# Branch B weights of three heads as seven block products in place of eight

## The chip, the cores and the metric

The kernel runs on one core of a Trainium2 chip. The metric is device time in microseconds (us) of one execution. A measurement of this kernel tells a change of about 0.2% from none. PE is the matrix engine (TensorE), PEld its weight loads, DVE is VectorE, ACT is ScalarE, POOL is GpSimd, SP the engine that issues most of the DMAs.

## The reference, cut to what matters

One transformer layer on 512 tokens of 1024 features, in float32: two token mixers in parallel (branch A, a gated delta rule; branch B, a retention), a gated sum, an output projection, and an MLP. The change concerns branch B's last step, where the four heads' outputs of 512 features each are multiplied by one weight matrix of 2048 x 1024.

```
ob = chunk_retention(qb, kb, vb)                     # 4 heads x 512 features
ob = rmsnorm(ob, norm_b.reshape(B_HEADS, B_DV)) * jax.nn.silu(gb...)
yb = ob.reshape(b, s, B_V) @ w_br_b                  # [512, 2048] @ [2048, 1024]
mix = (sigmoid(gate_a) * ya + sigmoid(gate_b) * yb) @ w_out
```

## The kernel before

Every matrix product is made of three matmuls: both operands are split into a rounded part `hi` and the rest `lo`, and hi x hi, hi x lo and lo x hi are added up in PSUM. A weight block of 128 x 1024 elements is loaded to a tile `raw`, ACT writes `whi` (L148), and DVE writes `wlo = raw - whi` (L149). `whi` and `wlo` have three buffers each, `raw` has two in each of two pools that take turns.

Stages in order of time: branch A to about 490 us; then four heads of branch B; then gate B, the last head's weights and the output projection to about 1034 us; then the MLP in four groups.

A head h of branch B runs through three functions. `scores(h, rows)` makes Q (48 matmuls), then, for h > 0, turns the rows of head h-1 to features (`features`, L397 transposes on PE into the one PSUM tile `tr`, `split_from` at L382 on ACT and L383 on DVE writes `og`, hi and lo), then K (48 matmuls), each followed by the rotation (L1540 to L1548: four products that read PSUM, two sums, then hi on ACT and lo on DVE, into `qr` and `kr`), then the 24 matmuls of the scores, which read `qr` and `kr` and write PSUM tiles `dl` (three buffers). Then the weights of head h-1: `branch_partial` makes two halves of 512 columns with `token_major`, 48 matmuls each, into the four PSUM tiles `mm`; each result is copied or added to `acc`. Then `outputs(h)` makes values and gates with `seven`.

`seven` is a product by blocks in which seven block products replace eight (Winograd's form). Its sums of weight blocks are made in DRAM beforehand: `BlockSums` copies a block (SP queue) and adds another to it by an accumulating DMA (POOL queue, L135). These jobs are issued one at a time behind weight loads, whenever the planned PE time has moved on by `JOB_US`; between 860 and 985 us of planned time (`REST`) none is. The tile library's scheduler sets the order of the instructions on each engine from their order in the code, priorities and free buffers; each engine then works through its own list.

Of the kernel before, what the change touches and what calls it, by code (L numbers as in the profile page):

```python
# [19 lines left out]
P = 128  # L20
T = 512
# [4 lines left out]
OFF_BA = 6144  # L26
OFF_QB, OFF_KB, OFF_VB, OFF_GB = 6160, 7184, 8208, 10256
OFF_GA, OFF_GBR = 12304, 13328
JOBS_FROM, JOB_US = 70.0, 8.5
SMALL_US, CONV_US, TOK_US, PK_US, INV_US, DB_US = 10.5, 6.5, 2.5, 2.0, 46, 1.2  # L30
VT_US, KS_US, PX_US, PC_US, GATE_US, FEAT_US, INV_PRIO, CONV_PRIO, SMALL_PRIO, KEY_PRIO, DECAY_US, AHEAD, TR_US, REC_PRIO, OUT_PRIO, SUM_PRIO = 2.5, 2.4, 3.5, 2.4, 11.0, 1.0, 0, 600, 800, 600, 20.0, 700, 2.2, 900, 900, 300
DFF = 4096
# [31 lines left out]
def hybrid_block_kernel(ctx: ExitStack, tc: tile.TileContext, a: dict, out: bass.AP):  # L64
    nc = tc.nc
    x_d = a["x"][0]
    w_in = a["w_in"][0]
    w_br = [a["w_br_a"][0], a["w_br_b"][0]]
# [6 lines left out]
    trickle, later_adds = [], []  # L75
# [79 lines left out]
    class BlockSums:  # L155


        def __init__(self, src, c1, c2, tag, full=True):
            def block(kh, c):
                return src[4 * kh * P : 4 * (kh + 1) * P, c : c + 512].rearrange("(k p) c -> p k c", p=P)  # L160
# [3 lines left out]
            self.t = {i: dr.tile([P, 4, 512], F32, tag=f"{tag}{i}", name="sums", bufs=1) for i in self.made}  # L164
            self.parts = []
            trickle.extend((self, i, k) for i in self.made for k in (0, 2))
# [4 lines left out]
        def adds(self):  # L171

            for i, k in ((2, 0), (1, 0), (3, 0), (2, 2), (1, 2), (3, 2), (0, 0), (0, 2)):
                if i not in self.made:
# [53 lines left out]
    def bank(pool):  # L228
        if pool is psx:
            return [psx.tile([P, T], F32, tag="dl", name="dl", bufs=3) for _ in range(2)]  # L230
        return [psm.tile([P, T], F32, tag="mm", name="mm") for _ in range(2)]
# [68 lines left out]
        times(d, "s4", x, True)  # L300
        out(0, 1, d, p1, ALU.add)

    def token_product(quarters, tokens=(0, 1)):

        pinned = []

        def product(pss, x, ks, wts, first):
            wh, wl = wts
            xh, xl = quarters[x]
            for t in tokens:  # L310
                tt = slice(t * P, (t + 1) * P)
                for kk in range(2):
                    k = 2 * ks + kk
                    lhs, rhs = (xh[:, k, tt], xl[:, k, tt]), (wh[:, kk, :], wl[:, kk, :])
                    tick(1536)
                    for i in range(3):
                        m = nc.tensor.matmul(  # L317
                            pss[t], lhs[i // 2], rhs[i % 2],
                            start=first and k + i == 0, stop=k + i == 5, skip_group_check=not first,
                        )  # L320
# [26 lines left out]
    def token_major(src, lhs, c0, kts, krow0=0):  # L347

        pss = [psm.tile([P, T], F32, tag="mm", name="mm") for _ in range(4)]
        for k0 in range(0, kts, 2):  # L350
            wh, wl = weights(src, krow0 + k0, 2, c0, 512)
            for t in range(4):
                tt = slice(t * P, (t + 1) * P)
                for kk in range(2):
                    kt = k0 + kk
                    mm3(
                        pss[t],
                        [x[:, tt] for x in lhs(kt)],
                        (wh[:, kk, :], wl[:, kk, :]),
                        kt == 0,  # L360
                        kt == kts - 1,
                    )
        return pss
# [32 lines left out]
    def transpose(ps, src):  # L396
        nc.tensor.transpose(ps, src, ident)  # L397
# [64 lines left out]
    with tc.tile_pool(name="xp", bufs=2) as xp:  # L462
# [405 lines left out]
    def gated_features(o_t, norms, tb=None):  # L868
# [8 lines left out]
    def branch_partial(w, og, krow0):  # L877
        for half in range(2):
            yield half, token_major(w, lambda kt: [o[:, kt, :] for o in og], half * 512, 4, krow0)

    class Rows2:
        def __init__(self, parts):
# [45 lines left out]
    def acc_rows(t, half):  # L928
        return acc_t[:, t, half * 512 : half * 512 + 512]
# [578 lines left out]
    with tc.tile_pool(name="pb", bufs=1) as pb_:  # L1508
# [41 lines left out]
        def scores(h, rows):  # L1550
            dec = pb_.tile([P, T], F32, tag="dec", name="dec", bufs=2)
            nc.scalar.dma_start(dec, a["c_decay"][h])
            pss = feature_major(w_in, xs, OFF_QB + h * 256, 256, 8)
            og = features(h - 1, rows) if rows else None
            qs, ks = (pb_.tile([P, 2, 2, T], F32R, tag=nm, name=nm) for nm in ("qr", "kr"))
            qs, ks = [qs[:, 0], qs[:, 1]], [ks[:, 0], ks[:, 1]]
            rotary(pss, qs)
            rotary(feature_major(w_in, xs, OFF_KB + h * 256, 256, 8), ks)
            if h == 0:
                ya_marks.append(ya_partial(3, prev))  # L1560
            scs = []
            sall = pb_.tile([P, 2560], F32R, tag="s", name="s")
            done = 0
            for i in range(4):
                t0 = min(i * P, 256)
                n = T - t0
                ps = psx.tile([P, T], F32, tag="dl", name="dl", bufs=3)
                for kk in range(2):
                    mm3(
                        ps[:, :n],  # L1570
                        [ks[j][:, kk, i * P : (i + 1) * P] for j in range(2)],
                        [qs[j][:, kk, t0:T] for j in range(2)],
                        kk == 0,
                        kk == 1,
                    )
# [9 lines left out]
            return scs, og  # L1585

        def features(h, rows):
            return gated_features(rows, lambda f: nb[:, 4 * h + f : 4 * h + f + 1])
# [47 lines left out]

        rows = None
        for h in range(4):
            scs, og = scores(h, rows)
            if h == 0:  # L1640

                def gate_a(t, half, src):
                    ta = tmp("g_t")
                    nc.scalar.activation(ta, src, AF.Tanh, scale=0.5)
                    dst = acc_rows(t, half)
                    nc.vector.scalar_tensor_tensor(dst, ta, 1.0, dst, ALU.add, ALU.mult)

                raw_pools.append((pb_, "ych"))
                gate_unit(ga_sums, OFF_GA, gate_a)
                for t in range(4):  # L1650
                    nc.scalar.dma_start(ya_d[:, t, :], acc_t[:, t, :])
# [385 lines left out]
```

## Time and profile before

| | |
|---|---|
| median of 3 runs | 1326.77 us (1326.51 to 1328.75) |
| profiled execution | 1326.62 us |
| its span, first to last instruction | 1324.8 us |
| PE busy | 1308.9 us (99%) |
| DVE busy | 931.3 us (70%) |
| ACT busy | 668.7 us (50%) |
| POOL busy | 89.7 us (7%) |
| DMA | 223.16 MB |

Time outside the span is 1326.62 - 1324.8 = 1.8 us. A busy PE is work in a pipe: a matmul of 512 columns shows as 390 ns, while one starts about every 227 ns.

### The profile page before, as it was taken

Reading aid. Unit: us, or ns where it says so; the run is one execution under the profiler, and the core shown is the slowest. Engines: PE = TensorE matmul, PEld = TensorE weight load, DVE = VectorE, ACT = ScalarE, POOL = GpSimd, SP = SyncE. Lnnn points to the kernel's source line nnn. Section 1 sums busy time; section 2 is a strip of 40 time slices with the busy share of each in tenths; the row PEclk is TensorE's granted clock in tenths of the full one; section 3 lists DMA queues with packets and bytes.
Section 4 is the critical chain, followed back from the end, with each engine's and each line's share of the span. In section 5 each row is a group of like instructions: output and inputs, shape, how many; then the busy total and the mean of one; then the engine's idle time right before and its main releaser. Section 6 shows DMA issues by size and latency. Waiting matters only on the chain.

```text
span 1324.8 us, 17530 instructions
## 1 busy us (share of the span) xinstructions
PE 1308.9 (99%) x6591; PEld 1085.9 (82%) x6591; DVE 931.3 (70%) x1560; ACT 668.7 (50%) x1168; POOL 89.7 (7%) x95
## 2 busy tenths in 40 slices
PE   9999999999999999999999999999999999999997
PEld 7888787888888878888888888888889888888886
DVE  6889757486666578876567776789685746637478
ACT  5784546455534533544453443465266636355364
POOL 2100100000000001000010000000001000000001
PEclk9999999999999999999999999999999999999999
DMA  5336952476765568887293462545629895859635
GB/s 192 134 112 160 203 132 64 114 181 174 191 161 133 127 178 179 271 253 153 79 260 105 120 214 64 160 157 175 223 82 247 230 256 156 245 154 251 191 119 135
DMA packets 115557, 223.16 MB, mean 168 GB/s; under 512 B 6982, under 2 KB 38896, under 8 KB 114960
## 3 DMA queue, kind: packets, MB, share of 16 engines
q1 hardware_dynamic: 96496, 175.13, 41.3%
q0 software_dynamic: 16944, 40.54, 19.1%
q10 hardware_dynamic: 2032, 6.36, 1.3%
q8 instruction: 52, 0.85, 0.3%
q14 instruction: 33, 0.27, 0.1%
HBM read 216.75 MB, written 72.37 MB: 218 GB/s over the span
## 4 chain that ended last, share of the span: by engine, by line
PE 89%; DVE 6%; ACT 3%; issue 1%; DMA 1%; DVEq 0%; ACTq 0%
PE mm L668 18%; PE mm L317 17%; PE dl L317 11%; PE mm L93 10%; PE mm L95 10%; PE mm L94 10%; PE dl L668 5%; PE tr L397 1%; DVE wlo L149 1%; PE dl L94 1%; PE dl L95 1%; PE dl L93 1%; PE tr L677 1%; PE mm L632 1%; DVE tmp L1061 1%
## 5 line engine op out<-in xcount | busy, mean ns | idle before, releaser
L149 DVE TENSOR_TENSOR wlo<-raw,whi 128x1024 fp32r<-128x1024 f32 x269 | 328.2, 1222 | 204.2 <-ACT whi L148 203.1
L148 ACT CAST whi<-raw 128x1024 fp32r<-128x1024 f32 x269 | 282.6, 1052 | 356.5 <-PE mm L668 71.7
L668 PE MATMUL mm<-actT,whi 128*128 128x512 f32 x448 | 144.5, 403 | 0.0
L317 PE MATMUL mm<-whi,xsum 128*128 128x512 f32 x384 | 120.6, 390 | 0.0
L95 PE MATMUL mm<-hn,wlo 128*128 128x512 f32 (+1 forms) x288 | 105.4, 366 | 0.0
L94 PE MATMUL mm<-hn,whi 128*128 128x512 f32 (+1 forms) x288 | 105.3, 366 | 0.0
L93 PE MATMUL mm<-hn,whi 128*128 128x512 f32 (+1 forms) x288 | 105.3, 366 | 0.0
L668 PEld LDWEIGHTS mm<-actT,whi 128*128 128x128 f32 x448 | 80.6, 188 | 14.8
L668 PE MATMUL mm<-actT,wlo 128*128 128x512 f32 x224 | 87.7, 392 | 0.0
L317 PEld LDWEIGHTS mm<-whi,xsum 128*128 128x128 f32 x384 | 71.8, 188 | 14.9
L317 PE MATMUL mm<-wlo,xsum 128*128 128x512 f32 x192 | 74.8, 390 | 0.0
L317 PE MATMUL dl<-whi,ffq 128*128 128x512 f32 x224 | 71.3, 389 | 0.0
L668 PE MATMUL mm<-whi,og 128*128 128x512 f32 x192 | 62.3, 397 | 0.0
L95 PEld LDWEIGHTS mm<-hn,wlo 128*128 128x128 f32 x288 | 54.3, 189 | 8.8
L93 PEld LDWEIGHTS mm<-hn,whi 128*128 128x128 f32 x288 | 54.3, 189 | 8.7
L94 PEld LDWEIGHTS mm<-hn,whi 128*128 128x128 f32 x288 | 54.3, 189 | 8.7
L668 PE MATMUL mm<-whi,actT 128*128 128x512 f32 x176 | 60.3, 405 | 1.0 <-DVE qf L906 1.0
L317 PE MATMUL dl<-whi,actT 128*128 128x512 f32 x192 | 61.1, 390 | 0.0
L317 PE MATMUL mm<-whi,ffq 128*128 128x512 f32 x192 | 60.9, 389 | 0.0
L1830 DVE TENSOR_TENSOR ffq<-r,ffq 128x512 fp32r<-128x512 f32 (+1 forms) x64 | 39.2, 621 | 28.0 <-ACT ffq L1830 27.9
L135 POOL DMA_DIRECT2D sums<-in_w_in_dram x28 | 32.6, 1164 | 359.8 <-DMA sums<-in_w_in_dram 359.8
L93 PE MATMUL mm<-actT,whi 128*128 128x512 f32 x128 | 51.5, 402 | 0.0
(394 smaller groups left out, 2839.4 us busy)
## 6 DMA issues: line engine op xcount, KB each, us to landing
raw<-in_w_in_dram SPq DMA_DIRECT2D x95, 512.0 KB, 4.9
raw<-sums SPq DMA_DIRECT2D x64, 512.0 KB, 4.4
raw<-in_w_up_dram SPq DMA_DIRECT2D x36, 512.0 KB, 7.2
sums<-in_w_in_dram SPq DMA_DIRECT2D x32, 512.0 KB, 5.2
sums<-in_w_down_dram SPq DMA_DIRECT2D x32, 512.0 KB, 6.9
sums<-in_w_in_dram POOLq DMA_DIRECT2D x28, 512.0 KB, 7.4
raw<-in_w_down_dram SPq DMA_DIRECT2D x24, 512.0 KB, 5.9
sums<-sums POOLq DMA_DIRECT2D x20, 512.0 KB, 8.5
```

The costliest lines, as they stand in the source:

```text
L93: nc.tensor.matmul(ps, lh, rh, start=first, stop=False)
L94: nc.tensor.matmul(ps, lh, rl, start=False, stop=False)
L95: nc.tensor.matmul(ps, ll, rh, start=False, stop=last)
L135: tc.keep_in_program_order(nc.gpsimd.dma_start(dst, src, accum_op=ALU.add))
L148: nc.scalar.copy(hi[:, :n], raw[:, :n])
L149: nc.vector.tensor_tensor(lo[:, :n], raw[:, :n], hi[:, :n], ALU.subtract)
L317: m = nc.tensor.matmul(pss[t], lhs[i // 2], rhs[i % 2], start=first and k + i == 0, stop=k + i == 5, skip_group_check=not first,)
L397: nc.tensor.transpose(ps, src, ident)
L632: pin(nc.tensor.matmul(first_keys[f][:, 256:512], ws[w][:, kk, :], xs[x][:, 2 * j + kk, 256:512], start=False, stop=kk == 1 and i == 2, sk ...
L668: m = tc.keep_in_program_order(nc.tensor.matmul(*args, **kwargs))
L677: tc.keep_in_program_order(nc.tensor.transpose(ps, src, ident if by is None else by))
L1830: return nc.scalar.copy(dst[0], r), nc.vector.tensor_tensor(dst[1], r, dst[0], ALU.subtract)
```

## The change

For heads 0, 1 and 2, `branch_partial` is replaced by `branch_seven`. The head's 512 features and 1024 output columns are cut in two, the 512 tokens too, so that a block product is 256 tokens x 256 features x 512 columns, 12 matmuls. Seven of them make the 84 matmuls of a head, where there were 96. Each takes a weight block of its own (7 splits into `whi` and `wlo` for 4), and its PSUM is added to `acc` before the next product goes to the same tiles (14 operations of 128 x 512 for 8). Two of the seven weight blocks are sums from DRAM, two are summed on DVE (`plus`).

The rows by features leave PSUM as float32 into `full` (ACT alone), which has the buffer of `kr`. From it hi and lo of three quarters (`11`, `12`, `22`, in `og`) and four sums of quarters with their hi and lo (`s1` to `s4`, in `osum`, which have the buffers of `vr`) are made. Head 3 stays as it was.

Six copy jobs and six add jobs come into the list, between those of the heads, and `JOB_US` goes from 8.5 to 7.8.

```diff
-JOBS_FROM, JOB_US = 70.0, 8.5
+JOBS_FROM, JOB_US = 70.0, 7.8
...
-    vg_sums = [BlockSums(w_in, OFF_VB + h * 512, OFF_GB + h * 512, f"vg{h}", False) for h in range(4)]
+    vg_sums, br_sums = [], []
+    for h in range(4):
+        vg_sums.append(BlockSums(w_in, OFF_VB + h * 512, OFF_GB + h * 512, f"vg{h}", False))
+        if h < 3:
+            br_sums.append(BlockSums(w_br[1][4 * h * P : 4 * (h + 1) * P, :], 0, 512, f"br{h}", False, 2))
...
-    for sums in [z_sums, ga_sums] + vg_sums + [gb_sums] + down_sums:
+    in_turn = [s for pair in itertools.zip_longest(vg_sums, br_sums) for s in pair if s]
+    for sums in [z_sums, ga_sums] + in_turn + [gb_sums] + down_sums:
...
-            og = features(h - 1, rows) if rows else None
+            xq = branch_quarters(h - 1, rows) if rows else None
...
+        def branch_quarters(h, rows):
+            full = pb_.tile([P, 4, T], F32, tag="kr", name="full")
+            og = [act.tile([P, 4, T], F32R, tag="og", name="og") for _ in range(2)]
+            sums = [pb_.tile([P, 2, 2, 2, 256], F32R, tag=f"vr{i}", name="osum") for i in range(2)]
+            for f in range(4):
+                ps = psx.tile([P, 4, P], F32, tag="tr", name="tr", bufs=1)
+                for t in range(4):
+                    transpose(ps[:, t, :], rows.feature(t, f))
+                n = 4 * h + f
+                nc.scalar.activation(
+                    full[:, f, :], ps.rearrange("p t c -> p (t c)"), AF.Copy, scale=nb[:, n : n + 1]
+                )
...
+            def halved(name, src, pair):
+                nc.scalar.copy(pair[0], src)
+                nc.vector.tensor_tensor(pair[1], src, pair[0], ALU.subtract)
...
+            for name, src, kh, th in (("11", a11, 0, 0), ("12", a12, 1, 0)):
+                halved(name, src, [part(w, kh, th) for w in og])
+            xq["22"] = [part(w, 1, 1) for w in og]
+            nc.scalar.copy(xq["22"][0], a22)
+            nc.vector.tensor_tensor(xq["22"][1], a22, xq["22"][0], ALU.subtract)
+            nc.vector.tensor_tensor(a22, a21, a22, ALU.subtract)
+            nc.vector.tensor_tensor(a21, a11, a21, ALU.subtract)
+            nc.vector.tensor_tensor(a11, a22, a11, ALU.subtract)
+            nc.vector.tensor_tensor(a12, a12, a11, ALU.add)
+            for i, src in ((2, a11), (1, a22), (3, a21), (4, a12)):
+                w = sums[(i - 1) // 2][:, (i - 1) % 2]
+                halved(f"s{i}", src, [w[:, 0], w[:, 1]])
...
+        def branch_seven(h, xq):
+            sums, product = br_sums[h], token_product(xq, kts=2)
...
+            x, y = sums.first_raw(1, 0), sums.raw(3, 0)
+            a = bank(psx)
+            times(a, "11", x, True)
+            add(0, 0, a, new=True)
+            plus(x, y)
+            v = sums.first_raw(3, 0)
+            b = bank(psm)
+            times(b, "12", v, True)
+            add(0, 0, b)
+            plus(v, x)
+            times(a, "s2", x, False)
+            add(0, 1, a, ALU.subtract, new=True)
+            w = sums.raw(1, 0)
+            c = bank(psm)
+            times(c, "s1", w, True)
+            add(1, 1, c, new=True)
+            times(a, "s3", y, False)
+            add(1, 1, a, ALU.subtract)
+            w = sums.first_raw(2, 0)
+            times(c, "s4", w, False)
+            add(0, 1, c)
+            times(a, "22", v, False)
+            add(1, 0, a, new=True)
...
-                for half, pss in branch_partial(w_br[1], og, 4 * (h - 1)):
-                    for t in range(4):
-                        dst = acc_rows(t, half)
-                        if h == 1:
-                            nc.scalar.copy(dst, pss[t])
-                        else:
-                            nc.vector.tensor_tensor(dst, dst, pss[t], ALU.add)
+                branch_seven(h - 1, xq)
```

`bank(psx)` takes two of the three `dl` tiles, which the scores use too; `bank(psm)` takes two of the four `mm` tiles. Lines below the new code move on by 80 or more.

PE before, in head 1, at the start of the scores. `mm` with `og` is the branch product of head 0, `dl` with `qr` and `kr` the scores:

```order
L95 MATMUL mm_5600<-whi_5605,og_5430 128x512
L93 MATMUL mm_5600<-whi_5605,og_5429 128x512
L94 MATMUL mm_5600<-wlo_5606,og_5429 128x512
L95 MATMUL mm_5600<-whi_5605,og_5430 128x512
L93 MATMUL dl_5554<-qr_5459,kr_5460 128x512
L94 MATMUL dl_5554<-qr_5459,kr_5460 128x512
```

PE after, at the same place. `mm_5504` with `actT` is the second PSUM tile of K:

```order
L95 MATMUL mm_5504<-actT_118,wlo_5540 128x512
L93 MATMUL mm_5504<-actT_118,whi_5539 128x512
L94 MATMUL mm_5504<-actT_119,whi_5539 128x512
L95 MATMUL mm_5504<-actT_118,wlo_5540 128x512
L93 MATMUL dl_5582<-qr_5487,kr_5488 128x512
L94 MATMUL dl_5582<-qr_5487,kr_5488 128x512
L95 MATMUL dl_5582<-qr_5487,kr_5488 128x512
```

Between K and the scores there stood 18 matmuls of the branch product, and now there is none; all 84 of the new product stand behind the scores. The same holds in heads 2 and 3.

DVE before, in head 1, from the last reading of K's PSUM to the first score. `ro` is the rotation, `kr` its low half, `sc` a score:

```order
L1542 TENSOR_TENSOR ro_5540<-mm_5476,rope_4327 128x512
L1543 TENSOR_TENSOR ro_5542<-mm_5476,rope_4327 128x512
L149 TENSOR_TENSOR wlo_5675<-raw_5671,whi_5674 128x1024
L1544 TENSOR_TENSOR ro_5539<-ro_5539,ro_5540 128x512
L1545 TENSOR_TENSOR ro_5541<-ro_5541,ro_5542 128x512
L1548 TENSOR_TENSOR kr_5460<-ro_5539,kr_5460 128x512
L1548 TENSOR_TENSOR kr_5460<-ro_5541,kr_5460 128x512
L1579 TENSOR_TENSOR sc_5561<-dl_5554,dec_5363 128x512
```

DVE after, the same stretch (`full` are the sums of quarters, `osum` their low halves):

```order
L1543 TENSOR_TENSOR ro_5568<-mm_5504,rope_4337 128x512
L1544 TENSOR_TENSOR ro_5570<-mm_5504,rope_4337 128x512
L149 TENSOR_TENSOR wlo_5677<-raw_5626,whi_5676 128x1024
L1620 TENSOR_TENSOR full_5440<-full_5440 128x2x256
L1609 TENSOR_TENSOR osum_5443<-full_5440,osum_5443 128x512
L1621 TENSOR_TENSOR full_5440<-full_5440 128x2x256
L1609 TENSOR_TENSOR osum_5443<-full_5440,osum_5443 128x512
L1609 TENSOR_TENSOR osum_5444<-full_5440,osum_5444 128x512 x2
L1545 TENSOR_TENSOR ro_5567<-ro_5567,ro_5568 128x512
L1546 TENSOR_TENSOR ro_5569<-ro_5569,ro_5570 128x512
L1549 TENSOR_TENSOR kr_5488<-ro_5567,kr_5488 128x512
L1549 TENSOR_TENSOR kr_5488<-ro_5569,kr_5488 128x512
```

Six operations on quarters came between the reading of K's PSUM and the sums of the rotation. Over the whole stretch from the first reading of Q's PSUM to the second `kr`, DVE has 32 operations for 23: four of `og` from PSUM (L383) went; two `plus` of 128 x 1024 and eleven on quarters came.

More of the change, by code (lines that the diff above doesn't have):

```diff
@@ L155, in hybrid_block_kernel, with __init__ @@
     class BlockSums:
-        def __init__(self, src, c1, c2, tag, full=True):
+        def __init__(self, src, c1, c2, tag, full=True, kts=4):
             def block(kh, c):
-                return src[4 * kh * P : 4 * (kh + 1) * P, c : c + 512].rearrange("(k p) c -> p k c", p=P)
+                return src[kts * kh * P : kts * (kh + 1) * P, c : c + 512].rearrange("(k p) c -> p k c", p=P)
             self.w12, self.first = block(0, c2), [block(0, c1), block(0, c1), block(1, c2), block(1, c1)]
             self.made = (2, 1, 3, 0) if full else (2, 0)
-            self.t = {i: dr.tile([P, 4, 512], F32, tag=f"{tag}{i}", name="sums", bufs=1) for i in self.made}
-            self.parts = []
-            trickle.extend((self, i, k) for i in self.made for k in (0, 2))
+            self.t = {i: dr.tile([P, kts, 512], F32, tag=f"{tag}{i}", name="sums", bufs=1) for i in self.made}
+            self.parts, self.kts = [], kts
+            trickle.extend((self, i, k) for i in self.made for k in range(0, kts, 2))
         def copy(self, i, k):
@@ L173, in adds @@
             for i, k in ((2, 0), (1, 0), (3, 0), (2, 2), (1, 2), (3, 2), (0, 0), (0, 2)):
-                if i not in self.made:
+                if i not in self.made or k >= self.kts:
                     continue
@@ L301, in seven, with token_product @@
         out(0, 1, d, p1, ALU.add)
-    def token_product(quarters, tokens=(0, 1)):
+    def token_product(quarters, tokens=(0, 1), kts=4):
         pinned = []
@@ L318, in product @@
                             pss[t], lhs[i // 2], rhs[i % 2],
-                            start=first and k + i == 0, stop=k + i == 5, skip_group_check=not first,
+                            start=first and k + i == 0, stop=k + i == kts + 1, skip_group_check=not first,
                         )
@@ L875, in gated_features @@
         return og
-    def branch_partial(w, og, krow0):
-        for half in range(2):
-            yield half, token_major(w, lambda kt: [o[:, kt, :] for o in og], half * 512, 4, krow0)
     class Rows2:
@@ L1584, in scores, with part @@
                 scs.append((sh, sl))
-            return scs, og
+            return scs, xq
+        def branch_quarters(h, rows):
[10 more added lines that the diff above has]
+                )
+            def part(w, kh, th):
+                return w[:, 2 * kh : 2 * kh + 2, 256 * th : 256 * th + 256]
+            xq = {}
+            def halved(name, src, pair):
+                nc.scalar.copy(pair[0], src)
+                nc.vector.tensor_tensor(pair[1], src, pair[0], ALU.subtract)
+                xq[name] = pair
+            a11, a12, a21, a22 = (part(full, kh, th) for kh, th in ((0, 0), (1, 0), (0, 1), (1, 1)))
+            for name, src, kh, th in (("11", a11, 0, 0), ("12", a12, 1, 0)):
[10 more added lines that the diff above has]
+                halved(f"s{i}", src, [w[:, 0], w[:, 1]])
+            return xq
@@ new lines, in branch_seven, with times, plus, add @@
+        def branch_seven(h, xq):
+            sums, product = br_sums[h], token_product(xq, kts=2)
+            def times(pss, x, raw, first):
+                product(pss, x, 0, split_weights(raw, 1024, 2), first)
+            def plus(dst, other):
+                with tc.high_priority(SUM_PRIO):
+                    nc.vector.tensor_tensor(dst, other, dst, ALU.add)
+            def add(th, ch, parts, op=ALU.add, new=False):
+                with tc.high_priority(400):
+                    for t in range(2):
+                        dst = acc_rows(2 * th + t, ch)
+                        if not new or h:
+                            nc.vector.tensor_tensor(dst, dst, parts[t], op)
+                        elif op is ALU.add:
+                            nc.scalar.copy(dst, parts[t])
+                        else:
+                            nc.scalar.mul(dst, parts[t], -1.0)
+            x, y = sums.first_raw(1, 0), sums.raw(3, 0)
[21 more added lines that the diff above has]
+            add(1, 0, a, new=True)
@@ L1638, in hybrid_block_kernel @@
         for h in range(4):
-            scs, og = scores(h, rows)
+            scs, xq = scores(h, rows)
             if h == 0:
```

## The prediction, made before the changed kernel ran

> **What bounds the kernel now.** First the head of the page, then its chain of waits:
>
> ```profile
> span 1324.8 us, 17530 instructions
> ...
> PE 1308.9 (99%) x6591; PEld 1085.9 (82%) x6591; DVE 931.3 (70%) x1560; ACT 668.7 (50%) x1168; POOL 89.7 (7%) x95
> ...
> PE 89%; DVE 6%; ACT 3%; issue 1%; DMA 1%; DVEq 0%; ACTq 0%
> ```
>
> PE is busy nearly the whole span and carries 89% of the chain. So fewer matmuls shorten the time, one for one, as long as nothing makes PE wait. Head 1 of branch B by stages (time stretch, then busy time of PE, PEld, DVE, ACT, POOL with counts, granted PE clock, DMA share):
>
> ```profile
> 592.00:616.00 24.00, 24.00 (x115) 19.79 (x115) 15.94 (x31) 10.56 (x18) 2.01 (x2) 1.00 0.75 154
> 616.00:642.00 26.00, 26.00 (x123) 21.81 (x122) 12.00 (x18) 11.20 (x17) 0.85 (x1) 1.00 0.42 95
> 642.00:687.00 45.00, 45.00 (x201) 37.26 (x200) 35.47 (x41) 23.02 (x30) 3.12 (x3) 1.00 0.70 201
> ```
>
> The stages are Q and K; scores and branch product; values and gates. PE never waits here. DVE is busy 15.9 of 24 us in the first, so there is room on average; whether there is room at the point where PE needs a result is a matter of the order. That point is the start of the scores, which need `kr`, the end of K's rotation. PE there, by start, duration and line:
>
> ```profile
> 603.39 0.60 PE L397 MATMUL tr<-cmat,o 128*128 128x128 f32 x4
> 603.74 0.47 PE L93 MATMUL mm<-actT,whi 128*128 128x512 f32 x1
> ...
> 606.80 0.60 PE L397 MATMUL tr<-cmat,o 128*128 128x128 f32 x4
> ...
> 615.92 0.39 PE L95 MATMUL mm<-actT,wlo 128*128 128x512 f32 x1
> 616.15 0.39 PE L93 MATMUL mm<-whi,og 128*128 128x512 f32 x1
> ...
> 620.24 0.40 PE L93 MATMUL dl<-qr,kr 128*128 128x512 f32 x1
> ```
>
> K's last matmul starts at 615.92. From 616.15 to 620.24 stand 18 matmuls of the branch product, (620.24 - 616.15) / 18 = 0.227 us each, and then the scores. DVE and ACT meanwhile:
>
> ```profile
> 604.35 0.69 ACT L382 ACTIVATE og<-tr,vecs 128x512 fp32r<-128x512 f32 x1
> 607.44 0.69 ACT L382 ACTIVATE og<-tr,vecs 128x512 fp32r<-128x512 f32 x1 [2.40 <-PE tr L397]
> ...
> 612.02 0.69 ACT L382 ACTIVATE og<-tr,vecs 128x512 fp32r<-128x512 f32 x1 [0.66 <-PE tr L397]
> 612.60 1.13 ACT L1547 CAST qr<-ro 128x512 fp32r<-128x512 f32 x2
> ...
> 619.40 1.23 ACT L1547 CAST kr<-ro 128x512 fp32r<-128x512 f32 x2 [2.23 <-DVE ro L1544]
> ```
>
> ```profile
> 604.79 1.22 DVE L149 TENSOR_TENSOR wlo<-raw,whi 128x1024 fp32r<-128x1024 f32 x1
> 605.92 0.75 DVE L383 SCALAR_TENSOR_TENSOR og<-tr,vecs,og 128x512 fp32r<-128x512 f32 x1
> 606.59 0.68 DVE L1544 TENSOR_TENSOR ro<-ro 128x512 f32<-128x512 f32 x1
> 607.19 0.68 DVE L1545 TENSOR_TENSOR ro<-ro 128x512 f32<-128x512 f32 x1
> ...
> 616.35 0.69 DVE L1542 TENSOR_TENSOR ro<-mm,rope 128x512 f32<-128x512 f32 x1 [0.47 <-PE mm L95]
> ...
> 619.29 0.68 DVE L1545 TENSOR_TENSOR ro<-ro 128x512 f32<-128x512 f32 x1
> 620.06 1.29 DVE L1548 TENSOR_TENSOR kr<-ro,kr 128x512 fp32r<-128x512 f32 x2
> ```
>
> The high half of `kr` is begun at 619.40 and the low half at 620.06; the scores start at 620.24. So the 18 matmuls cover the rotation almost to the tenth: without them PE would stand from 616.15 to about 620. That cover is the thing to watch.
>
> **The change part by part.**
>
> *Matmuls.* 96 become 84 in each of three heads: 12 x 0.227 = 2.72 us less per head, 8.2 us in all, on the path.
>
> *The start of the scores.* In the new order no branch matmul stands between K and the scores (the first product takes `dl` tiles, which the scores use first). PE still ends K at about 616.2, since Q, K and the four sets of transposes are the same number. When is `kr` ready? The starts above give DVE's step: 1.13 us for 128 x 1024 (604.79 to 605.92), 0.60 for 128 x 512 (606.59 to 607.19).
>
> ACT copies `tr` to `full` from 604.35; each further set of transposes waits for the copy before it, so the copies come every 1.4 us (0.64 from the start of a set to ACT's, 606.80 to 607.44; 0.58 for the copy, 612.02 to 612.60; some 0.15 for the signal back), and the fourth ends at 604.35 + 3 x 1.4 + 0.6 = 609.1. Behind it ACT makes the high half of `qr`; DVE's low half can follow 0.66 us after its start (as 619.40 and 620.06 show), at 609.8. From 604.79 DVE now goes through five operations of 128 x 1024 (three `wlo`, two `plus`) and 21 of 128 x 512 before the second sum of K's rotation is done: 5 x 1.13 + 21 x 0.60 = 18.3 us. It waits 0.9 us for `qr` (it would be there at 608.9) and about 0.05 us at each of six operations on its own last result: 19.5 us, to 624.3. K's PSUM, read from 617.0, is not late for it. The first sum is done 0.6 earlier, at 623.7; ACT then makes the high half of `kr`, to 624.4 (it could not earlier in any case, since `full` has the same buffer and is read until 623.1). PE starts the scores at 624.5, waits for the low halves again inside the first six matmuls (625.1 and 625.7 by the step of 0.60), which costs 0.1 more. PE thus stands 624.5 - 616.2 = 8.3 us, with the rest 8.4 us per head. The neighbours: 7.0 if the waits inside are nothing and the casts are quick, 10 if signals cost as much again; I take 8.4.
>
> *PE's clock.* The stand is longer than any in this trace but the ends. The start and the end show what a stand does:
>
> ```profile
> 1.19 3.60 PE L475 MATMUL warm<-warm 128*128 128x512 bf16 x8 [1.19 <-DVE warm L464]
> 5.42 2.98 PE L475 MATMUL warm<-warm 128*128 128x512 bf16 x10
> ...
> 1316.00:1317.00 1.00, 0.90 (x4) 0.40 (x3) 0.71 (x5) 0.15 (x1) 0.00 (x0) 1.00 1.25 143
> ...
> 1320.00:1321.00 1.00, 0.00 (x0) 0.00 (x0) 0.93 (x4) 0.00 (x0) 0.00 (x0) 0.95 1.02 330
> 1321.00:1322.00 1.00, 0.00 (x0) 0.00 (x0) 0.73 (x2) 0.00 (x0) 0.00 (x0) 0.50 0.58 219
> ```
>
> The last matmul ends at 1316.9, and the granted clock is 0.95 in 1320 to 1321 and 0.50 from 1321: half, 4 us after. A stand of 8.3 us is twice that, so the scores begin at half speed. At the start of the span the first eight matmuls take 3.60 / 8 = 0.45 us each, the next ten 0.30 on average: cold for some 4 to 5.5 us. At half speed every cold microsecond loses half: 2.0 to 2.75 us; part of it falls into the waits for `kr`, and PE may warm sooner. I take 1.5 per head, between 0 and 2.75. [...]
>
> *Splits, sums and adds in the branch product.* Durations (busy, mean ns after the comma, then idle before):
>
> ```profile
> L149 DVE TENSOR_TENSOR wlo<-raw,whi 128x1024 fp32r<-128x1024 f32 x269 | 328.2, 1222 | 204.2 <-ACT whi L148 203.1
> L148 ACT CAST whi<-raw 128x1024 fp32r<-128x1024 f32 x269 | 282.6, 1052 | 356.5 <-PE mm L668 71.7
> L1895 DVE TENSOR_TENSOR facc<-facc,dl 128x512 f32<-128x512 f32 x22 | 14.5, 679 | 0.0
> L135 POOL DMA_DIRECT2D sums<-in_w_in_dram x28 | 32.6, 1164 | 359.8 <-DMA sums<-in_w_in_dram 359.8
> ```
>
> A product is 12 x 0.227 = 2.72 us on PE. Against it stand one `wlo` (1.13) and two adds (2 x 0.60) on DVE, 2.33 us, and one `whi`, 1.05, on ACT. It fits, with little over; tiles `a` and `c` are used again after one other product, 2.72 us, and the adds take 1.2. Cost 0, bound 0.5 per head; the cover is PE's own work, and would be gone if DVE were another 0.4 us per product busier.
>
> *Loads.* Three more loads in all, and the block `v` now stays in its `raw` buffer until the split for the last product, some 13 us after the first begins (five products less the lead of a split). The second load for the values waits for that buffer on SP's queue, with those behind it.
>
> ```profile
> raw<-in_w_in_dram SPq DMA_DIRECT2D x95, 512.0 KB, 4.9
> ...
> raw<-in_w_up_dram SPq DMA_DIRECT2D x36, 512.0 KB, 7.2
> ```
>
> 13.4 + 4.9 + 2.3 for the split = 20.6 us after the first product's start; PE needs it at 7 x 2.72 + 2.72 = 21.8. With a landing of 7.2 us it would be 1.1 late. I take 0.3 per head, between 0 and 2.
>
> *Jobs.* Six copies and six adds more; POOL issues an add in 1.16 us and is 7% busy. Two adds of the second MLP group now stand behind POOL's wait for the residual rows (L1786); that group is used some 100 us later, so they cost nothing. Closer jobs leave the last ones within three loads of where they were. 0, give or take 1 us in all.
>
> *The sum.* Per head -2.72 + 8.4 + 1.5 + 0.3 = +7.5; three heads +22.4. The profiled execution took 1326.62 us (0.15 below the median of 1326.77), so 1349 us.
>
> **Rivals.**
>
> *Faster: the rotation stays covered.* If `kr` were ready within 2.7 us of K's end, the saved matmuls would decide. Then the time is 1326.6 - 8.2 = 1318.4. For it: DVE's busy share of 66% in that stage. Against it: six operations stand on DVE between K's PSUM and the sums, and `kr` has no buffer until the last of them.
>
> *The clock stays.* The stand is there, but the clock does not fall or PE is warm at once: 3 x (-2.72 + 8.4 + 0.3) = +17.9, 1344.5. For it: nothing in the trace shows a fall amid work. Against: the end of the span.
>
> *All the bad ends together in place:* cold for 5.5 us, loads 1 us late, a stand of 9.5: 3 x (-2.72 + 9.5 + 2.75 + 1) = +31.6, 1358.
>
> *Half covered.* The stand is only 2 to 4 us (DVE's idle in the stage swallows the new work): -2 to +4 us, 1325 to 1331. Against: the count of operations.
>
> *No change in the work:* not possible; the new order holds 84 matmuls per head.
>
> **How the numbers follow.** A difference under 0.2% (2.7 us) is no change. Chances: the forecast 0.55, the clock stays 0.20, the bad ends 0.13, faster 0.07, half covered 0.05. Slower takes in the first three and some of the last, 0.90; same 0.03; faster 0.07. The range from 1340 to 1359 leaves out the covered cases (0.12) and some 0.06 above; its low end is the stand at 7.0 without the clock, 3 x 4.6 = +13.8, 1340.4.
>
> **What would show it.** Right: in each of three heads, about 616, 708 and 800 us, PE idle before the first score matmul for some 8 us with ACT's `kr` as what ended it; granted clock under 1 just behind; the 84 matmuls then packed at 0.227. Wrong: no such idle time, or PE waiting in the branch product on `acc` or `wlo`, or a longer time with the clock at 1.00 throughout.

## The result and the profile after

After took 1358.73 us (median of 4, 1355.33 to 1362.24) against 1326.89 for before (median of 4, 1326.51 to 1328.75): ratio 1.0235, 95% interval [1.0219, 1.0251], slower by 31.8 us. The profiled execution took 1362.24 us, the longest of the four. Its page, with the chain's shares in the last line:

```profile
span 1359.8 us, 17583 instructions
...
PE 1313.7 (97%) x6555; PEld 1085.3 (80%) x6555; DVE 971.4 (71%) x1614; ACT 690.4 (51%) x1198; POOL 96.1 (7%) x101
...
PE 76%; DVE 11%; ACT 6%; DMA 5%; issue 2%; ACTq 0%; DVEq 0%
```

PE's share of the chain fell from 89% to 76%; DVE, ACT and DMA took it. PE issues 36 matmuls fewer (3 x 12), and yet its busy time grew by 4.8 us: some of them ran at a granted clock of 0.50, as the stretches below show. What PE waited for in all (us in total, times, longest), the three longest rows that before has no counterpart of:

```profile
PE dl L93 <- ACT kr L1548: 23.3, 3, 7.8
PE dl L673 <- ACT vt L1375: 2.9, 1, 2.9
PE mm L93 <- ACT r L1905: 1.8, 1, 1.8
```

The first row is the wait that the prediction named, in the three heads. The other two lie elsewhere: `vt` in the late gates of branch A at 350 us, `r` in the MLP at 1043 us. To split the 35.0 us between the spans (1359.8 - 1324.8), take the first set of transposes of `o`, which opens each head. PE's rows of after, then the first and the last of before:

```profile
610.40 0.27 PE L402 MATMUL tr<-cmat,o 128*128 128x128 f32 x1
711.47 0.38 PE L402 MATMUL tr<-cmat,o 128*128 128x128 f32 x2
813.16 0.38 PE L402 MATMUL tr<-cmat,o 128*128 128x128 f32 x2
912.89 0.27 PE L402 MATMUL tr<-cmat,o 128*128 128x128 f32 x1
```

```profile
603.39 0.27 PE L397 MATMUL tr<-cmat,o 128*128 128x128 f32 x1
...
883.92 0.27 PE L397 MATMUL tr<-cmat,o 128*128 128x128 f32 x1
```

The three heads took 302.5 us in place of 280.5, +22.0 (the sum on record said +22.4). Ahead of them after was already 7.0 us late, and behind them it lost another 35.0 - 7.0 - 22.0 = 6.0. These 13 us are what the prediction's sum, which gave the jobs 0, does not have. They are those of the longest execution; by the median it is 31.8 - 22.0 = 9.8 us.

The stand in head 1, PE and then what it waited for on DVE and ACT:

```profile
623.20 0.39 PE L95 MATMUL mm<-actT,wlo 128*128 128x512 f32 x1
631.37 0.80 PE L93 MATMUL dl<-qr,kr 128*128 128x512 f32 x1 [7.77 <-ACT kr L1548]
631.96 0.63 PE L94 MATMUL dl<-qr,kr 128*128 128x512 f32 x1
...
634.09 0.41 PE L93 MATMUL dl<-qr,kr 128*128 128x384 f32 x1
```

```profile
626.90 0.69 DVE L1609 TENSOR_TENSOR osum<-full,osum 128x512 fp32r<-128x512 f32 x1
627.51 0.69 DVE L1621 TENSOR_TENSOR full<-full 128x512 f32<-128x512 f32 x1
628.11 1.89 DVE L1609 TENSOR_TENSOR osum<-full,osum 128x512 fp32r<-128x512 f32 x3
629.91 0.69 DVE L1545 TENSOR_TENSOR ro<-ro 128x512 f32<-128x512 f32 x1
630.51 0.69 DVE L1546 TENSOR_TENSOR ro<-ro 128x512 f32<-128x512 f32 x1
```

```profile
630.69 1.17 ACT L1548 CAST kr<-ro 128x512 fp32r<-128x512 f32 x2 [1.84 <-DVE ro L1545]
```

PE idles 7.77 us. DVE goes from one operation to the next without a gap, the sums of quarters and their low halves ahead of K's rotation; ACT's cast of `kr` follows the first sum of the rotation. The first six score matmuls then take 634.09 - 631.37 = 2.72 us, twice 6 x 0.227. The clock in the three heads, for each from the end of K's last matmul to the fall, and from the first score matmul to the return (columns as in the prediction; PEclk is the third from the right):

```profile
623.60:627.40 3.80, 0.00 (x0) 0.00 (x0) 3.80 (x6) 1.74 (x3) 0.00 (x0) 1.00 0.00 0
631.37:634.23 2.86, 2.86 (x7) 2.24 (x8) 1.27 (x2) 0.49 (x1) 0.00 (x0) 0.50 0.01 3
...
724.68:729.80 5.12, 0.00 (x0) 0.00 (x0) 5.12 (x9) 2.48 (x4) 0.00 (x0) 1.00 0.24 65
732.44:736.63 4.19, 4.19 (x11) 3.57 (x12) 1.97 (x3) 0.99 (x2) 0.00 (x0) 0.50 0.01 4
...
826.37:828.79 2.42, 0.00 (x0) 0.00 (x0) 2.42 (x4) 1.37 (x2) 0.00 (x0) 1.00 0.00 0
834.13:839.03 4.90, 4.90 (x14) 4.28 (x15) 1.98 (x4) 1.12 (x2) 0.00 (x0) 0.50 0.00 0
```

The clock is full until 3.8, 5.1 and 2.4 us after PE's last matmul, half from there, and full again 2.9, 4.2 and 4.9 us after PE began. The same stand of 7.77 us thus costs each head another amount: half of the time that PE worked at half speed, 1.4, 2.1 and 2.5 us, 6.0 in all. With it the heads come to -8.2 + 23.3 + 6.0 = 21.1 of the 22.0 us; 0.9 is not assigned.

### The profile page after: what moved, and what is told of

Same layout as the page of the kernel before. It is cut to its first block, busy times and chain, and to the rows that moved or that the text cites. A ratio compares the mean times of both kernels' runs of the same rounds, so it can differ in the third digit from the quotient of the medians.

```text
span 1359.8 us, 17583 instructions
## 1 busy us (share of the span) xinstructions
PE 1313.7 (97%) x6555; PEld 1085.3 (80%) x6555; DVE 971.4 (71%) x1614; ACT 690.4 (51%) x1198; POOL 96.1 (7%) x101
## 4 chain that ended last, share of the span: by engine, by line
PE 76%; DVE 11%; ACT 6%; DMA 5%; issue 2%; ACTq 0%; DVEq 0%
PE mm L322 16%; PE mm L673 14%; PE dl L322 11%; PE mm L93 7%; PE mm L95 7%; PE mm L94 7%; PE dl L673 5%; DVE wlo L149 3%; DMA raw<-in_w_up_dram 2%; PE dl L93 2%; PE dl L94 1%; PE dl L95 1%; ACT whi L148 1%; PE tr L402 1%; DMA raw<-sums 1%
## 5 line engine op out<-in xcount | busy, mean ns | idle before, releaser
L148 ACT CAST whi<-raw 128x1024 fp32r<-128x1024 f32 x278 | 292.6, 1054 | 369.3 <-PE mm L322 90.1
L149 DVE TENSOR_TENSOR wlo<-raw,whi 128x1024 fp32r<-128x1024 f32 x278 | 339.9, 1223 | 195.0 <-ACT whi L148 194.4
```

The source lines that it names most:

```text
L148: nc.scalar.copy(hi[:, :n], raw[:, :n])
L149: nc.vector.tensor_tensor(lo[:, :n], raw[:, :n], hi[:, :n], ALU.subtract)
```

## The experiments

Times are medians; a ratio is against before, run on the same chip. "Heads" is the change of the three heads' periods together in the profiled execution, measured as above.

| run | us | ratio, 95% interval | heads, us |
|---|---|---|---|
| after | 1358.73 | 1.0235 [1.0219, 1.0251] | +22.0 |
| kr_free | 1359.64 | 1.0235 [1.0217, 1.0252] | +22.5 |
| warm | 1353.82 | 1.0192 [1.0179, 1.0206] | +16.6 |
| late | 1351.96 | 1.0183 [1.0164, 1.0203] | +13.9 |
| fill | 1349.27 | 1.0150 [1.0127, 1.0174] | +12.5 |
| fill_late | 1346.53 | 1.0139 [1.0111, 1.0166] | +10.6 |
| fast | 1345.42 | 1.0136 [1.0121, 1.0152] | +12.1 |
| fast_lean | 1329.99 | 1.0017 [1.0009, 1.0026] | -1.1 |
| jobs | 1335.88 | 1.0059 [1.0044, 1.0074] | 0.0 |
| jobs85 | 1333.99 | 1.0047 [1.0029, 1.0066] | -0.1 |
| pace | 1331.35 | 1.0017 [1.0003, 1.0031] | 0.0 |
| jobs_mid | 1333.46 | 1.0042 [1.0024, 1.0061] | -0.1 |
| jobs_clear | 1330.98 | 1.0024 [1.0015, 1.0033] | 0.0 |

### What holds kr: a buffer of its own for full

```diff
-            full = pb_.tile([P, 4, T], F32, tag="kr", name="full")
+            full = pb_.tile([P, 2560], F32, tag="s", name="full")[:, :2048].rearrange("p (f c) -> p f c", f=4)
```

> After, with the gated rows full in the buffer of the score matrix s in place of kr's, so that kr's high half no longer waits until the sums have read full; every engine's instructions stand in the same order as in after. Order theory (DVE's 32 operations set when kr is ready, and the buffer adds nothing): stand 7.6 to 7.9 us per head, 1357 to 1360 us. Rival (the buffer holds kr back): the stand ends at least 1 us earlier in each head, 1355 us or less.

The wait is the same:

```profile
PE dl L93 <- ACT kr L1548: 23.1, 3, 7.7
```

So the shared buffer costs nothing beside DVE's order. The prediction had the order's bound 0.6 us behind the buffer's (623.7 and 623.1), too close to tell from its sum alone.

### What the clock costs: matmuls in the stand

```diff
+            else:
+                ps = psm.tile([P, T], F32, tag="mm", name="mm")
+                for n in range(32):
+                    nc.tensor.matmul(ps, qs[n % 2][:, 0, :P], qs[0][:, 0, :], start=True, stop=True)
```

> After, with 32 more matmuls of qr by qr in each of the three heads between K and the scores, into a PSUM tile that nothing reads: 7.3 us at 0.227, so PE is busy in the stand. The scores can start no earlier. Clock theory (slow clock behind the stand costs 1.5 us per head, 0 to 2.75): granted clock 1.00 through 616:650, first score matmuls at 0.23 in place of 0.80, 1358.7 - 4.5 = 1354 us (1350.5 at the least). Rival (the clock costs nothing that kr would not have cost): 1358 to 1360 us.

PE in head 1, and its stretch:

```profile
620.70 7.42 PE L1565 MATMUL mm<-qr 128*128 128x512 f32 x32
628.62 0.50 PE L93 MATMUL dl<-qr,kr 128*128 128x512 f32 x1 [0.50 <-ACT kr L1548]
```

```profile
616.00:650.00 34.00, 33.50 (x155) 27.84 (x154) 26.86 (x40) 16.18 (x24) 0.00 (x0) 1.00 0.32 100
```

The scores begin no earlier after K (7.9 us), but the clock is 1.00 and the heads take 22.0 - 16.6 = 5.4 us less, 1.8 per head; the median is 4.9 below after's. Clock theory holds; the 6.0 us read from after's trace is near it. The prediction took 1.5 per head. From fall to return the half-speed stretches of after last 6.83, 6.83 and 10.24 us; they begin after 3.80, 5.12 and 2.42 us without a matmul.

### DVE's order: the sums behind K's rotation

`late` also has `kr_free`'s buffer.

```diff
+            yield xq
             nc.scalar.copy(xq["22"][0], a22)
...
             rotary(feature_major(w_in, xs, OFF_KB + h * 256, 256, 8), ks)
+            if rows:
+                next(rest)
```

> After, with full in the buffer of s (which alone moved nothing) and the quarter sums written behind K's rotation, so that six of DVE's operations (the last two sums of quarters and four low halves) no longer stand ahead of kr's two sums: the order on PE is that of after. Order theory: kr 6 x 0.6 = 3.6 us sooner, stand 4.0 to 4.6 us in place of 7.8 in each head, less slow clock too: 1358.7 - 3 x (3.6 to 4.6) = 1345 to 1348 us, unless the sums, now behind the scores, come late for the third product (up to 3 us per head back, on osum). Rival (ACT's casts or K's PSUM hold kr): stand over 6.5 us, 1354 us or more.

```profile
PE dl L93 <- ACT kr L1548: 12.7, 3, 4.2
...
626.24 0.80 PE L93 MATMUL dl<-qr,kr 128*128 128x512 f32 x1 [4.22 <-ACT kr L1548]
...
626.24:631.64 5.40, 5.40 (x15) 4.36 (x16) 4.92 (x9) 1.77 (x3) 0.00 (x0) 0.50 0.24 93
```

The stand fell to 4.2 us as forecast, which shows DVE's order as its cause. The time missed the forecast by 4 us or more, in part because the shorter stand cost the clock more, not less: the half-speed stretch of head 1 lasts 6.83 us, as in after (624.81 to 631.64), but now 5.40 us of it fall on PE's work, a loss of 2.7 us in place of 1.4. In the three heads it is 8.3 us (half of 5.40, 5.53 and 5.61) in place of 6.0. So of the 10.6 us that left the wait 8.3 should come out, and the heads gained 8.1.

### Cover: two banks changed, alone and with the late sums

`fill` changes the banks; `fill_late` adds the two edits of `late`.

```diff
-            a = bank(psx)
+            a = bank(psm)
...
-            c = bank(psm)
+            c = bank(psx)
             times(c, "s1", w, True)
```

> After, with the branch product's tiles a and b taken from the mm banks and c from the dl banks (the other way round in after), so that the first 24 to 34 matmuls of the branch product can stand between K and the scores (5.4 to 7.7 us of cover). Stand theory (7.8 us of stand and 1 to 2 us of slow clock per head): PE's wait on kr shrinks to 0 to 2 us per head, granted clock 1.00 behind K, 1358.7 - 3 x (7 to 9) = 1332 to 1338 us. Rival (the loss is DVE's 32 operations, and comes back as waits in the branch product wherever PE takes its matmuls): 1345 us or more, with PE waiting on wlo, osum or acc in the branch product for over 3 us per head.

> Both: sums behind K's rotation and tiles a and b in the mm banks, so that 22 matmuls of the branch product (5.0 us) stand between K and the scores and the scores stand ahead of the product with the sums. Stand theory: 4.2 us of need against 5.0 of cover, no wait on kr, granted clock 1.00; what is left is the saved matmuls and the jobs: 1328.2 - 8.2 + 7.7 = 1328 us, 1325 to 1333 with small waits. Rival (DVE's operations come due one product later, and PE waits on osum behind the scores, as in the run with the banks changed): 1336 to 1345 us with 3 to 5 us on osum per head.

PE's waits in 600 to 910 us, of `fill`, and then of `fill_late`:

```profile
PE mm L322 <- ACT osum L1608: 7.4, 2, 3.7
PE mm L322 <- DVE osum L1609: 3.2, 1, 3.2
```

```profile
PE dl L93 <- ACT kr L1548: 7.4, 2, 3.7
PE mm L322 <- ACT osum L1611: 1.7, 1, 1.7
```

In `fill` no wait on `kr` is left: its place is taken by one of 3.2 to 3.7 us per head on `osum`, the sums for the third product. That is the rival's mechanism and its time. With the sums late, `kr` is late again in two heads, 3.7 us each: in head 2 four `acc` and three `wlo` operations of the early products stand on DVE between the readings of K's PSUM and the rotation's sums. Neither theory had this wait for `fill_late`, and the time is above both ranges. Cover moves the wait: by a product in `fill`, and here back to `kr`.

### All cures together, and DVE's share alone

`fast` is `fill_late` with the rotation of K under a high priority and the jobs paced by place (`JOB_US` back at 8.5):

```diff
-            rotary(feature_major(w_in, xs, OFF_KB + h * 256, 256, 8), ks)
+            pss = feature_major(w_in, xs, OFF_KB + h * 256, 256, 8)
+            with tc.high_priority(900 if rows else 0):
+                rotary(pss, ks)
...
-        queued[0] += JOB_US
+        queued[0] += 7.1 if 478 < queued[0] < 1000 else JOB_US
```

> The branch product by seven with all that the runs so far point to: quarter sums behind K's rotation and full in the buffer of s, tiles a and b in the mm banks, jobs paced by place (8.5, then 7.1 from 478 to 1000), and K's rotation written with a priority of 900, so that no acc, wlo or osum stands on DVE between its sums and kr's low halves. If DVE's order is what cost (about 15 matmuls of cover, 3.4 us, against a need of 3.5 to 4.5; some 0.5 to 1 us on osum): 3 x (-2.72 + 1 to 2) and 0 to 2 us for jobs: 1321 to 1328 us, the period of a head 92.5 to 94 us in place of 94.2, no clock under 1 in the heads. Rival (DVE simply has no room for nine operations more between the transposes and the scores, whatever their order): waits of 3 us or more per head come back on osum or sc, 1332 us or more.

`fast_lean` takes DVE work away (`plus` does nothing, and the low halves are not made). Its jobs go out as in `jobs_clear` below, not as in `fast`; either way of sending them moved the heads of before by 0.1 us or less.

```diff
-                halved(f"s{i}", src, [w[:, 0], w[:, 1]])
+                nc.scalar.copy(w[:, 0], src)
+                xq[f"s{i}"] = [w[:, 0], w[:, 0]]
```

> The version with all cures (K's rotation first, sums late, two banks changed) and the jobs sent as in the run beside it, with part of the branch product's preparation left out: the four low halves osum of the sums (the high halves stand in for them) and the two sums of weight blocks. It computes another result and shows DVE's share alone: 4 x 0.6 + 2 x 1.13 = 4.7 us of DVE per head less, matmuls and their order the same. Theory of room (DVE has no place for the new operations between the transposes and the third product): the periods of a head, 97.1, 99.4 and 96.1 us there, fall by 4 to 6 us to 91.5 to 94, the waits on osum to under 0.5 us, 1326 us or less. Rival (PE waits for something else than DVE's time, such as ACT's casts or PSUM tiles): periods above 95 us, 1333 us or more.

PE's waits in the heads and the stretch behind head 2's transposes, of `fast`:

```profile
PE mm L322 <- ACT osum L1613: 9.2, 3, 3.7
PE mm L322 <- DVE osum L1614: 1.4, 1, 1.4
...
700.00:735.00 35.00, 31.31 (x139) 24.88 (x138) 32.08 (x49) 16.66 (x26) 1.66 (x2) 0.90 0.44 106
```

and of `fast_lean`:

```profile
PE dl L322 <- ACT whi L148: 2.2, 1, 2.2
...
700.00:735.00 35.00, 35.00 (x166) 28.58 (x165) 32.06 (x48) 18.72 (x28) 3.15 (x3) 1.00 0.72 152
...
831.29 2.94 ACT L148 CAST whi<-raw 128x1024 fp32r<-128x1024 f32 x3 [7.38 <-DMA raw<-in_w_in_dram]
```

With `kr` free of its wait, PE still stands on `osum`, with DVE busy 32.1 of 35 us. Take 4.7 us of DVE's work per head away, and PE is busy 35.00 of 35.00. DVE is as busy as in `fast`, but beside 166 matmuls in place of 139. ACT's casts of the sums, which end most of the waits in `fast`, are still there, so they alone were not what held PE. PE also no longer needs the results left out; DVE's time and that need are not told apart. The first two heads take 91.8 and 92.0 us, close to the 94.2 - 2.72 = 91.5 that the saved matmuls allow. So the saving is real, and DVE has no room for what buys it there, in any of the orders that were tried: after has (971.4 - 931.3) / 3 = 13.4 us of DVE more per head. The third head took 95.7 us, where before took 92.0, for a reason of its own: ACT waited 7.38 us for a load of the values' weights, and PE for ACT. What delayed that load was not tested. With that, the 1326 us or less expected of the theory of room did not come; two heads bear it out, the time does not.

### The jobs

Five kernels have before's matmuls in before's heads and differ in the list of jobs. `jobs` has after's list and pace, `jobs85` the list at the old pace, `pace` the old list at the new pace:

```diff
+            br_sums.append(BlockSums(w_br[1][4 * h * P : 4 * (h + 1) * P, :], 0, 512, f"br{h}", False, 2))
...
-JOBS_FROM, JOB_US = 70.0, 8.5
+JOBS_FROM, JOB_US = 70.0, 7.8
```

> The kernel before, with the six copies and six adds for branch B's three blocks in the list of jobs and JOB_US at 7.8, as after has them; nothing reads these sums, and all products are those of before. Theory A (the prediction: jobs cost 0, give or take 1 us): 1326 to 1328 us. Theory B (what the three heads' stands leave unexplained is the jobs: they push z's sums and loads back in the late gates at 320 to 365 us, and loads in the MLP): 1333 to 1337 us, with PE waiting in 320:365 for weights or what hangs on them some 5 to 6 us more than before.

> The kernel before with JOB_US at 7.8 in place of 8.5 and nothing else: the 59 copies and adds of before come closer together. The list with the closer pace cost 7.7 us in the run with the jobs alone. Theory P (the pace moves z's copies and adds against the late gates' own loads): 1333 to 1337 us, PE waiting in 345:370 as there. Theory L (it takes the six copies and six adds more): 1326 to 1330 us, no new wait of PE.

> The kernel before with the six copies and six adds in the list (their sums unread) and JOB_US left at 8.5: the other half of the pair. Theory P (the pace is what costs): 1326 to 1330 us. Theory L (the added jobs cost, by the transfers that they put on the queues): 1333 us or more. At 8.5 the last jobs come 12 x 8.5 = 102 us later than before, so PE waiting late in the MLP for the down products' sums would be a third outcome, of its own place (after 1100 us).

The jobs alone cost 7.7 us by the medians, the time of theory B. The profile shows two places. The late gates, 345 to 370 us, of `before` and then of `jobs`; with each the waits of ACT for loads that lead to it, and PE's:

```profile
345.00:370.00 25.00, 25.00 (x113) 20.94 (x112) 12.59 (x19) 12.21 (x24) 2.27 (x2) 1.00 0.66 184
...
340.91 1.05 ACT L148 CAST whi<-raw 128x1024 fp32r<-128x1024 f32 x1 [2.26 <-DMA raw<-in_w_in_dram]
```

```profile
345.00:370.00 25.00, 23.08 (x96) 19.18 (x97) 13.57 (x19) 14.82 (x31) 2.28 (x2) 0.93 0.63 171
...
345.09 1.04 ACT L148 CAST whi<-raw 128x1024 fp32r<-128x1024 f32 x1 [6.21 <-DMA raw<-in_w_in_dram]
...
346.92 1.13 PE L673 MATMUL dl<-st,kf 128*128 128x256 f32 x4 [2.00 <-ACT vt L1379]
```

ACT waits 6.21 us for one load, and `vt`, which PE needs, stands behind that cast on ACT. In `jobs85` and in `pace` this place is whole (PE 25.00 of 25.00), so it comes from the pace with the longer list. The other profiles bear this out, with a spread: of the seven kernels with after's list and pace, six show PE's wait on `vt` (1.4 to 4.2 us) and `fill` does not; of the other seven none does. The second place is the start of the MLP, seen best where the first is cured. `jobs_mid` and `jobs_clear` pace by place, the first as `fast` does; the second also sends adds ahead of copies from 690 on (its edit):

```diff
-        queued[0] += JOB_US
+        queued[0] += 6.5 if 478 < queued[0] < 860 else JOB_US
...
-            if ready and (added[0] or not trickle):
+            if ready and (added[0] or not trickle or 690 < queued[0] < 1000):
```

> The kernel before with the same twelve jobs more (sums unread), but paced by place: 8.5 until the planner's clock shows 478, 7.1 from there to 1000 (the heads, where the transfer engines have room), 8.5 behind. So z's and ga's jobs keep their places of before in the late gates, and by 1000 the list is as far as in before. Theory of place (the jobs cost 4 us where the closer pace meets the late gates at 345:370, and 3 to 5 us where the list runs late against the up loads at 1005:1030): 1327 to 1330 us, and no new wait of PE in either stretch. Rival (twelve transfers of 0.5 MB more cost it wherever they stand): 1332 to 1336 us, with the time gone in the heads.

> The kernel before with the twelve jobs more (sums unread), 8.5 apart until 478, 6.5 from there to 860, 8.5 behind, and from 690 on an add that may go is sent ahead of the next copy. So when POOL reaches its wait for the residual rows, 53 adds are out of 54 copies, where before had 43 of 50 and the kernel with the jobs paced by place 47 of 55: one add is left to go off when that wait ends, in place of 7 and 8. Theory of the burst (POOL's pent-up adds leave together at 990 to 1030 us and hold up the first up loads, 12.0 us to land in place of 6.6): PE busy 1005:1030 as in before, up loads under 8 us, 1326 to 1329 us. Rival (the added transfers cost their time wherever they are): 1332 to 1336 us, with the loss in the heads or later in the MLP.

The up loads issued in 995 to 1030 us (median us to landing, last) and the stretch behind, in `before`, `jobs_mid` and `jobs_clear`; for `jobs_mid` also ACT and PE:

```profile
raw<-in_w_up_dram SPq DMA_DIRECT2D x4, 512.0 KB, 6.6
...
1005.00:1030.00 25.00, 25.00 (x140) 21.90 (x139) 13.33 (x18) 15.12 (x27) 4.30 (x4) 1.00 1.05 255
```

```profile
raw<-in_w_up_dram SPq DMA_DIRECT2D x4, 512.0 KB, 12.0
...
1005.00:1030.00 25.00, 21.26 (x117) 18.60 (x117) 7.74 (x9) 10.36 (x20) 5.15 (x5) 0.86 0.95 220
...
1015.97 1.04 ACT L148 CAST whi<-raw 128x1024 fp32r<-128x1024 f32 x1 [7.15 <-DMA raw<-in_w_up_dram]
...
1017.35 0.80 PE L93 MATMUL mm<-hn,whi 128*128 128x512 f32 x1 [3.74 <-ACT r L1830]
```

```profile
raw<-in_w_up_dram SPq DMA_DIRECT2D x4, 512.0 KB, 4.1
...
1005.00:1030.00 25.00, 25.00 (x143) 22.06 (x143) 12.96 (x17) 14.66 (x27) 1.14 (x1) 1.00 0.68 190
```

POOL issues adds in order, and in `before` it idles 154.25 us ahead of the residual rows and 40.82 us ahead of the load of `post`; both hold back the adds that come behind. From 989 us on these leave one after another among the up loads, with the transfer engines at 0.95 to 1.05. By the order of the programs before has 7 such adds and no loss, `jobs_mid` 8 and a loss, and `jobs_clear`, with 1, none: the up loads land in 4.1 us. The number alone does not decide: `jobs85` has 7 as before, of later groups, with up loads at 14.4 us and PE busy 21.81 of 25.00. What differs is how many go at once: in `before` single adds at 988.96 and 998.43 beside the up loads, in `jobs_mid` two at 999.97 and 1000.52, in `jobs85` four from 988.25 to 990.25 (`pace` has two at 989.00, and no loss). In the profiles up loads of 4.1 to 8.0 us (8.0 in `pace`) go with no loss, and of 10.1 to 14.4 us (10.1 in `jobs`) with one. `jobs_clear`'s profile bears out that the adds delay the loads; that it depends on adds side by side is a reading, not tested.

`jobs_mid` cured the first place and not the second, so its time missed the theory of place; nothing was lost in the heads, so its rival is out too.

Not settled: `jobs_clear` gained only part in the median (+4.1 us where `jobs` has +7.7), outside its theory's range and its rival's. Its profiled execution, at 1328.03 us, is the shortest of its 12, and shows no loss; what the others (up to 1334.28) lose, no profile shows. `pace` spreads in the same way, 1326.73 (profiled, without a wait) to 1334.81. The verdict on theory P or L is therefore both: the list cost 6.1 us by the medians without the pace, and the pace 3.4 without the list.

## Why the prediction was right in its sign and short in its size

The time was forecast at 1349 us and came at 1358.73, inside the range and 9.7 above the point. The heads' sum, +22.4 for +22.0, is that close partly by luck: per head the stand and the loads were set 0.9 us too high, the clock 0.5 too low, and 0.3 is not assigned.

- *Matmuls*, -2.72 per head: as said. `fast_lean` shows the gain wherever nothing else stands in its way.
- *The stand*, 8.4 per head: 7.77 measured in head 1, and 23.3 in all. The cause was right: DVE's order, by `late`; not the buffer, by `kr_free`.
- *The clock*, 1.5 per head: 1.8, by `warm`, and 2.0 by after's trace (1.4 to 2.5). So the rival "the clock stays" is out.
- *Late loads*, 0.3 per head: 0 measured, since in 600 to 915 us PE waits for nothing but `kr`.
- *Splits, sums and adds*, 0: right for the block product itself, since its cover was there. It was right only because PE had already paid in the stand: when the stand was covered (`fill`, `fast`), the same DVE work came back as a wait on `osum`.
- *Jobs*, "0, give or take 1 us in all": wrong, 7.7 by `jobs` alone, and 2.1 of the 9.8 us outside the heads stay open. This is the term that was mis-sized. The step that failed is "that group is used some 100 us later, so they cost nothing": the adds behind POOL's wait were not late for their own use. By the profiles they were in the way of other transfers, which PE needed at once; and the closer pace was costed by where the last jobs land, not by what they meet in the late gates on the way.
- "All the bad ends together" gave 1358, the time that came, by luck: the stand was shorter than forecast, no load in the heads was late, and PE worked 2.9 to 4.9 us at half speed, not 5.5.

With the jobs at 7.7 the sum on record would have been 1357.

## What to carry to other kernels

Before saving matmuls at a place where PE is full, count the work that the next engine gets between the same two points: here 2.72 us of PE per head were bought with 13.4 us of DVE, most of it in a stretch of 50 us (592 to 642 in before) where DVE had 27.9 to do already, and every way that was tried of covering the wait moved it to another thing that DVE makes. Background transfers are not free because their data is wanted late (the added jobs alone cost 7.7 us here): cost them by what they run beside, and look for queues where a wait dams them up.

## What the runs showed of the hardware

In `fill_late` the clock fell without one long stand; no single wait in this part is over 1.7 us:

```profile
634.00:638.00 4.00, 1.71 (x8) 1.07 (x8) 3.73 (x8) 0.88 (x2) 0.00 (x0) 1.00 0.92 301
638.00:642.00 4.00, 3.64 (x9) 2.90 (x10) 2.18 (x5) 1.87 (x4) 0.00 (x0) 0.59 0.08 26
```

PE was busy 1.71 of 4 us in small pieces, and the granted clock was 0.59 in the next 4 us, though PE was busy for 3.64 of them. This is one case, and what set the moment of the fall is not shown.

What a stand cost in clock did not follow its length: one of 4.2 us (`late`) lost 2.7 to 2.8 us, one of 7.77 (after) 1.4 to 2.5. In after's profile the half-speed stretches amid work last 6.83, 6.83 and 10.24 us in the three heads, 3.41 us in the late gates (from 350.92) and 3.41 us in the MLP (from 1043.83). The loss is half of what of such a stretch fell on PE's work: 2.86 of 6.83 us in after's head 1, 5.40 in `late`'s.
